# Reordering the edges of a matmul kernel: where x is loaded and turned at the start, the order of products in the first group and of the last quarters, and the slots for C

## The chip, the cores and the metric

The kernel runs on one core of a Trainium2 chip. The metric is device time in microseconds (us), smaller is better. A time here is the median of several executions, with the lowest and highest beside it. "Span" is the length of the one execution that was profiled; it comes out about 1.8 us below the time of the same execution.

In the profile lines, PE is TensorE's matmuls, PEld its loading of weights, DVE is VectorE, ACT ScalarE, POOL GpSimd, SP SyncE; a q after the name is that engine's queue, and xN a count. The "granted clock" is the share of TensorE's full clock that the profile shows as granted; "half clock" is a stretch where it is 0.50. A "chance wait" is one that some profiles of the same code show and others do not.

## The reference, cut to what matters

```python
def setup_inputs():
    B, S, D = 8, 2048, 2048
    return {"x": randn(B, S, D) as float32, "w": randn(D, D) as float32}

def reference(x, w):
    cs = np.cumsum(x, axis=1)
    diff = cs - (cs shifted by one row)      # which is x again
    return np.matmul(diff, w)
```

So the result is x (16384 rows of 2048) times w (2048 x 2048), in blocks of 128 rows.

## The kernel before

Three stages matter. **The first rows:** while w comes in, three row blocks of x are multiplied directly in bf16. Their x is loaded in four quarters, cast, turned by TensorE (transposes through two banks of PSUM) and copied out, by ScalarE and VectorE in turn.

```python
        load_x(0)
        ...
            for ko in range(KO - KQ):
                if h == 0 and ko % KQ == 2:
                    load_x(ko // KQ + 1)
                fetch(h, ko)                      # a block of w
                if h == 0 and ko % KQ == 0 and ko == 0:
                    turn_x(0)                     # 3 turns: cast, 4 transposes, copy
                taken(h, ko)                      # ScalarE casts it, VectorE takes its maximum
                for r in range(EARLY):
                    plain(h, r, ko)               # 2 matmuls for each of 3 row blocks
                if h == 0 and ko % KQ == 2:
                    turn_x(ko // KQ + 1)
```

**The groups:** all other rows go in groups of four blocks, with a fast two-by-two scheme in fp16: sums S1 to S4 of pieces of x, differences T1 to T4 of pieces of w, and seven products instead of eight. The first group (`group_plain`) makes whole products; in later ones three of the products are split once more (`inner_product`). Results gather in four float32 slots of C, `a` to `d`: `keep` copies a product from PSUM into a slot (ScalarE), `add` adds one to it (VectorE), `put` writes it out (a DMA from SyncE's queue). The rows of a later group are prepared on the side: `fetch_x` loads 1 MB, `weigh` measures the row's size on ScalarE *using a slot of C as a waste bin*, `scale_of` inverts the measure on VectorE, `ready` narrows to fp16 on ScalarE, `turn` transposes by DMA. The helper `after` fixes the order on each engine to the order of the calls.

```python
        C22 = new_c(d)                      # in group_plain
        keep(C22, Z, vg)
        ready(g + 4)
        turn(g + 4)
        fetch_x(g + 5)
        product(X, A21g, T3, False)
        add(C22, X, vg)
        put(C22, g + 1, 1)
        ...
        put(C12g, g, 1)
        weigh(h + 4, b)
        scale_of(h + 4)
        ...
        less_in(*in3)
        for t, X, slot, v in ((g, X, c, vg), (h, Y, b, vh)):
            product(X, parts(t + 1)[1], T4, False)
            ...
            put(C21, t + 1, 0)
        fetch_x(g + 8)
```

**The tail:** in the last group the final two quarters are made of seven small products sharing banks; the very last step is one addition over a full width of 1024 and one 512 KB write.

## Time and profile before

1523.6 us, median of 3 runs (1523.51 to 1524.18). By stage, in the profiled execution (span 1520.0):

| stage | from..to, us | length | what sets its end |
|---|---|---|---|
| first rows | 0..61.90 | 61.90 | TensorE, with pauses for turning x |
| fourth row block | 61.90..83.36 | 21.46 | ScalarE, busy 21.46 |
| first group to the first product S3 x T3 of the second | 83.36..153.51 | 70.15 | TensorE, with waits |
| rest of the passage, to inner product A3 | 153.51..169.91 | 16.40 | TensorE |
| steady groups, up to the end of the last full-width product | 169.91..1507.62 | 1337.71 | TensorE, without a pause |
| tail | 1507.62..1520.04 | 12.42 | last addition, write, end |

How to read it: two stages have TensorE continuous or nearly so, and there only fewer matmuls could help. The order of instructions shows 6904 matmuls before and after the change, so what can be won lies in the pauses. The lines that carry this are in the prediction below.

### The profile page before, as it was taken

What the parts mean: (1) busy time and instruction counts of PE and PEld (TensorE: products, weight loads), DVE (VectorE), ACT (ScalarE), POOL (GpSimd) and SP (SyncE); (2) the same over time, 40 slices, a digit from 0 to 9 for tenths busy, and PEclk for the clock granted to TensorE, in tenths of its full rate; (3) what the DMA queues carried; (4) which work ended last, traced back from release to release, by engine and by line L of the source; (5) the groups of instructions that cost most, each with busy time, mean ns of one, the idle gap of its engine ahead of it and who ended that gap; (6) DMA issues with size and microseconds to landing.
All of it is one profiled execution on the core that took longest, in us unless ns stands there. A gap on an engine that the chain in (4) does not pass through costs nothing.

```text
span 1520.0 us, 19095 instructions
## 1 busy us (share of the span) xinstructions
PE 1494.0 (98%) x6900; PEld 674.3 (44%) x6904; DVE 1104.8 (73%) x2066; ACT 861.2 (57%) x1102; POOL 10.0 (1%) x21
## 2 busy tenths in 40 slices
PE   6999999999999999999999999999999999999998
PEld 3443444444444444444444444444444444444443
DVE  7996776767776767776767776767776767777767
ACT  5865555655555565555565555565556565556551
POOL 0200000000000000000000000000000000000000
PEclk9999999999999999999999999999999999999999
DMA  9968789879788888888787787778887877887772
GB/s 365 362 189 225 208 243 222 228 229 245 214 247 207 238 231 241 219 240 223 223 241 233 224 235 216 226 228 241 234 237 206 232 230 232 238 236 222 220 206 111
DMA packets 321326, 351.49 MB, mean 231 GB/s; under 512 B 266832, under 2 KB 266832, under 8 KB 305232
## 3 DMA queue, kind: packets, MB, share of 16 engines
q1 hardware_dynamic: 319952, 346.08, 79.1%
q0 software_dynamic: 1280, 4.20, 0.8%
q8 instruction: 54, 0.88, 0.2%
q14 instruction: 40, 0.33, 0.1%
HBM read 150.99 MB, written 134.22 MB: 188 GB/s over the span
## 4 chain that ended last, share of the span: by engine, by line
PE 90%; DVE 0%; issue 0%; ACT 0%; ACTq 0%
PE b L366 54%; PE b L377 36%; DVE c L413 0%; ACT c L408 0%; DVE u L497 0%; DVE m L111 0%; DVE s L112 0%; ACTq L408 0%
## 5 line engine op out<-in xcount | busy, mean ns | idle before, releaser
L413 DVE SCALAR_TENSOR_TENSOR c<-b,u,c 128x512 f32<-128x512 f32 (+1 forms) x882 | 674.8, 800 | 237.8 <-ACT c L408 115.0
L408 ACT ACTIVATE c<-b,u 128x512 f32<-128x512 f32 x496 | 315.1, 680 | 278.9 <-PE b L366 183.7
L366 PE MATMUL b<-W,xT 128*128 128x512 f16 x2048 | 462.4, 379 | 0.6 <-ACT c L408 0.6
L366 PE MATMUL b<-W,W 128*128 128x512 f16 x1764 | 414.6, 381 | 0.9 <-ACT c L408 0.7
L105 ACT ACTIVATE c<-fin 128x2048 f16<-128x2048 f32 x92 | 175.7, 1910 | 246.9 <-DMA out_dram<-c 227.9
L366 PEld LDWEIGHTS <-xT 128*128 128x128 f16 x2048 | 200.3, 98 | 242.6 <-issue 1.0
L366 PEld LDWEIGHTS <-W 128*128 128x128 f16 x2016 | 197.7, 98 | 244.6 <-issue 4.9
L116 ACT ACTIVATE fin<-fin,s 128x2048 f16<-128x2048 f32 x123 | 246.3, 2002 | 90.0 <-issue 47.0
L377 PEld LDWEIGHTS <-W 128*128 128x128 f16 x1560 | 152.2, 98 | 186.8 <-issue 1.1
L377 PE MATMUL b<-W,W 128*128 128x512 f16 x810 | 219.8, 379 | 0.8 <-DVE c L413 0.8
L377 PE MATMUL b<-W,xT 128*128 128x512 f16 x720 | 179.9, 379 | 0.0
L377 PE MATMUL b<-inner,W 128*128 128x512 f16 x660 | 176.6, 379 | 0.0
L377 PEld LDWEIGHTS <-xT 128*128 128x128 f16 x960 | 93.9, 98 | 113.3
L472 DVE TENSOR_REDUCE m<-m 128x1 f32<-128x4 f32 x29 | 4.5, 157 | 104.0 <-ACT b L464 104.0
L366 PE MATMUL b<-W 128*128 128x512 f16 x252 | 76.0, 381 | 2.6 <-DVE W L422 2.5
L464 ACT ACTIVATE b<-fin 128x512 f32<-128x512 f32 x116 | 68.1, 587 | 12.6 <-DMA fin<-in_x_dram 11.9
L422 DVE TENSOR_TENSOR W<-W,xT 128x1024 f16<-128x1024 f16 x122 | 68.1, 559 | 3.2
L422 DVE TENSOR_TENSOR W<-xT,W 128x1024 f16<-128x1024 f16 x122 | 67.3, 552 | 0.0
L377 PE MATMUL b<-inner,xT 128*128 128x512 f16 x240 | 61.6, 379 | 0.0
L422 DVE TENSOR_TENSOR W<-xT,xT 128x1024 f16<-128x1024 f16 (+1 forms) x92 | 54.7, 595 | 0.0
L111 DVE TENSOR_SCALAR m<-m 128x1 f32<-128x1 f32 x124 | 18.5, 149 | 44.9 <-ACT c L105 43.8
L212 PE MATMUL b<-wb,xP 128*128 128x512 bf16 x188 | 44.3, 392 | 6.1 <-ACT wb L204 5.9
(56 smaller groups left out, 471.7 us busy)
## 6 DMA issues: line engine op xcount, KB each, us to landing
fin<-in_x_dram SPq DMA_DIRECT2D x124, 1024.0 KB, 5.4
out_dram<-c SPq DMA_DIRECT2D x248, 512.0 KB, 3.2
W<-in_w_dram SPq DMA_DIRECT2D x32, 512.0 KB, 9.3
W<-in_x_dram SPq DMA_DIRECT2D x12, 256.0 KB, 7.7
xT<-fin SPq DMA_TRANSPOSE x184, 5.0
out_dram<-o POOLq DMA_DIRECT2D x10, 256.0 KB, 5.4
out_dram<-wb POOLq DMA_DIRECT2D x6, 256.0 KB, 9.7
xP<-in_x_dram SPq DMA_DIRECT2D x1, 1024.0 KB, 7.4
```

Source lines behind the costliest of these rows:

```text
L105: return m, nc.scalar.activation(waste.bitcast(f16), xf, ABS, scale=1.0 / ROW, accum_out=m)
L111: nc.vector.tensor_scalar(m, m, TINY, None, MAX)
L116: return xh, nc.scalar.activation(xh, xf, COPY, scale=s)
L212: nc.tensor.matmul(ps[r][n], xP[:, r, ko, :], wb[h, ko][:, ds(n * NB, NB)], start=(ko == 0), stop=(ko == KO - 1),)
L366: nc.tensor.matmul(ps[n], a[k], b[k][:, n, :], start=(first and k == 0), stop=(k == KH - 1), skip_group_check=True,)
L377: nc.tensor.matmul(ps, a[k], b[k], start=(first and k == 0), stop=(k == 3), skip_group_check=True)
L408: after("act", lambda: nc.scalar.activation(c, p, COPY, scale=scale))
L413: "dve", lambda: nc.vector.scalar_tensor_tensor(c, p, scale, c, MUL, ADD)
L422: after("dve", lambda: nc.vector.tensor_tensor(dst.all, p.all, q.all, op))
L464: lambda: nc.scalar.activation(ps[i % 2], xf[:, at], ABS, scale=1.0 / ROW, accum_out=m4[:, i : i + 1],),
L472: after("dve", lambda: nc.vector.tensor_reduce(m, m4, AX.X, ADD))
```

## The change

Its intent: let the loads of w go ahead of three quarters of x so that products start on more of w; fill the passage between the first groups so that no engine stands behind a wait which its next piece of work does not need; keep products that share a bank apart in the tail and write the end in two halves. Cut to its core:

```diff
-                if h == 0 and ko % KQ == 2:
-                    load_x(ko // KQ + 1)
+                if h == 0 and ko == KQ:
+                    for q in range(1, 4):
+                        load_x(q)
...
+                if h == 0 and KQ <= ko < KQ + 3:
+                    turn_x(ko - KQ + 1)
...
@@ group_plain
         put(C12g, g, 1)
-        weigh(h + 4, b)
+        product(X, A22g, T4, False)
+        C21 = new_c(b)
+        keep(C21, X, vg)
+        put(C21, g + 1, 0)
+        weigh(h + 4, a)
...
-        C22 = new_c(b)
+        C22 = new_c(d)
         keep(C22, Z, vh)
-        weigh(g + 5, d)
+        weigh(g + 5, b)
...
@@ group, where it follows group_plain
-            weigh(h + 1, d)
-            ready(h + 1)
...
-            less_in3(*in3)
+            weigh(h + 1, c)
+            ready(h + 1)
             less_in(*in4)
-            less_in3(*in4)
...
         inner_product(A2, in2, banks, C11g, C11h, *u, between_2)
+        if second:
+            less_in3(*in3)
+            less_in3(*in4)
...
@@ the last group only (four_last): the small products in another order, and
-            add(halves(C21h), both(q), vh)
-            put(C21h, h + 1, 0)
+            for n in range(2):
+                at = ds(n * NB, NB)
+                add(C21h[:, at], q, vh)
+                nc.scalar.dma_start(out2[ds((h + 1) * P, P), at], C21h[:, at])
@@ the driver
-        slots = a, d, b, c
+        slots = (b, d, a, c) if g == PLAIN else (a, d, b, c)
```

More of the change, by code (lines that the diff above doesn't have):

```diff
@@ L240 @@
             for ko in range(KO - KQ):
-                if h == 0 and ko % KQ == 2:
-                    load_x(ko // KQ + 1)
+                if h == 0 and ko == KQ:
+                    for q in range(1, 4):
+                        load_x(q)
                 fetch(h, ko)
-                if h == 0 and ko % KQ == 0 and ko == 0:
+                if h == 0 and ko == 0:
                     turn_x(0)
+                if h == 0 and KQ <= ko < KQ + 3:
+                    turn_x(ko - KQ + 1)
                 taken(h, ko)
@@ L248 @@
                     plain(h, r, ko)
-                if h == 0 and ko % KQ == 2:
-                    turn_x(ko // KQ + 1)
             for ko in range(KO - KQ, KO):
@@ L605, in group_plain @@
         put(C22, g + 1, 1)
+        A22h = parts(h + 1)[1]
         S3h = sums(h, S4h)
@@ L629, in group_plain @@
         ready(g + 5)
+        turn(g + 5)
         product(Z, S4h, B22, False)
@@ L632, in group_plain @@
         put(C12h, h, 1)
+        fetch_x(g + 8)
         less_in(*in3)
-        for t, X, slot, v in ((g, X, c, vg), (h, Y, b, vh)):
-            product(X, parts(t + 1)[1], T4, False)
-            C21 = new_c(slot)
-            keep(C21, X, v)
-            if t == g:
-                turn(g + 5)
-            put(C21, t + 1, 0)
-        fetch_x(g + 8)
+        product(Y, A22h, T4, False)
+        C21 = new_c(c)
+        keep(C21, Y, vh)
+        put(C21, h + 1, 0)
     def group(g, X, Y, Z, V, a, b, c, d):
@@ L728, in between_3, with seven, four, four_last @@
                 ready(g + 5)
+        def seven():
+            product(Y, S3h, T3, False)
+            add(C22, Y, vh)
+            put(C22, h + 1, 1)
+        def four():
+            a11, a12, a22, s1, s2, s3, s4 = A4
+            Q1, Q2, Q4, t11, Q3, t21, t22 = in4
+            C21g, C21h = new_c(b), new_c(c)
+            product_in(X[0], a12, t21, False)
+            product_in(q, a11, t11, True)
+            product_in(X[1], s4, t22, False)
+            keep(C21g, X, vg)
+            turn(g + 5)
+            fetch_x(g + 8)
+            add(C21g[:, :NB], q, vg)
+            product_in(e, s1, Q1, True)
+            add(C21g[:, NB:], e, vg)
+            product_in(Y[0], a22, Q4, False)
+            keep(C21h, Y, vh)
+            product_in(q, s2, Q2, False)
+            add(C21g[:, NB:], q, vg)
+            put(C21g, g + 1, 0)
+            weigh(h + 5, d)
+            if g + 4 < END:
+                product(X, parts(g + 4)[0], B11, True)
+            add(C21h[:, NB:], e, vh)
+            product_in(q, s3, Q3, False)
+            scale_of(h + 5)
+            for t in (g + 4, h + 4) if g + 4 < END else ():
+                units[t] = unit(t)
+            add(halves(C21h), both(q), vh)
+            put(C21h, h + 1, 0)
+            ready(h + 5)
+        def four_last():
+            a11, a12, a22, s1, s2, s3, s4 = A4
+            Q1, Q2, Q4, t11, Q3, t21, t22 = in4
+            C21g, C21h = new_c(b), new_c(c)
+            product_in(q, a11, t11, True)
+            keep(C21g[:, :NB], q, vg)
+            product_in(X[0], a12, t21, False)
+            add(C21g[:, :NB], X[0], vg)
+            product_in(X[1], s4, t22, False)
+            keep(C21g[:, NB:], X[1], vg)
+            product_in(e, s1, Q1, True)
+            add(C21g[:, NB:], e, vg)
+            keep(C21h[:, NB:], Y[1], vh)
+            add(C21h[:, NB:], e, vh)
+            product_in(q, s2, Q2, False)
+            add(C21g[:, NB:], q, vg)
+            put(C21g, g + 1, 0)
+            product_in(Y[0], a22, Q4, False)
+            keep(C21h[:, :NB], Y[0], vh)
+            product_in(q, s3, Q3, False)
+            for n in range(2):
+                at = ds(n * NB, NB)
+                add(C21h[:, at], q, vh)
+                nc.scalar.dma_start(out2[ds((h + 1) * P, P), at], C21h[:, at])
         inner_product(A3, in3, banks, C12g, C12h, *u, between_3)
@@ L733, in group @@
         two()
-        product(Y, S3h, T3, False)
-        add(C22, Y, vh)
-        put(C22, h + 1, 1)
-        a11, a12, a22, s1, s2, s3, s4 = A4
-        Q1, Q2, Q4, t11, Q3, t21, t22 = in4
-        C21g, C21h = new_c(b), new_c(c)
-        product_in(X[0], a12, t21, False)
-        product_in(q, a11, t11, True)
-        product_in(X[1], s4, t22, False)
-        keep(C21g, X, vg)
-        turn(g + 5)
-        fetch_x(g + 8)
-        add(C21g[:, :NB], q, vg)
-        product_in(e, s1, Q1, True)
-        add(C21g[:, NB:], e, vg)
-        product_in(Y[0], a22, Q4, False)
-        keep(C21h, Y, vh)
-        product_in(q, s2, Q2, False)
-        add(C21g[:, NB:], q, vg)
-        put(C21g, g + 1, 0)
-        weigh(h + 5, d)
-        if g + 4 < END:
-            product(X, parts(g + 4)[0], B11, True)
-        add(C21h[:, NB:], e, vh)
-        product_in(q, s3, Q3, False)
-        scale_of(h + 5)
-        for t in (g + 4, h + 4) if g + 4 < END else ():
-            units[t] = unit(t)
-        add(halves(C21h), both(q), vh)
-        put(C21h, h + 1, 0)
-        ready(h + 5)
+        seven()
+        (four if g + 4 < END else four_last)()
     fetch_x(PLAIN + 3)
```

## The prediction

> **What bounds the kernel now.** I read the page first, then one table of busy time by stage, then the timeline wherever that table shows TensorE short of work.
>
> ```profile
> PE 1494.0 (98%) x6900; PEld 674.3 (44%) x6904; DVE 1104.8 (73%) x2066; ACT 861.2 (57%) x1102; POOL 10.0 (1%) x21
> ```
>
> The table's columns are the stretch, its length, busy time of each engine, granted clock, DMA share, GB/s.
>
> ```profile
> 0.00:61.90 61.90, 48.65 (x236) 22.54 (x240) 48.18 (x64) 38.12 (x46) 4.20 (x12) 1.00 0.96 372
> 61.90:83.36 21.46, 18.76 (x80) 7.82 (x81) 20.98 (x42) 21.46 (x23) 3.68 (x7) 0.92 0.97 292
> 83.36:140.25 56.89, 56.07 (x257) 24.75 (x255) 41.35 (x90) 27.87 (x32) 2.15 (x4) 1.00 0.78 216
> 140.25:153.51 13.26, 10.02 (x34) 3.80 (x34) 11.79 (x37) 9.27 (x18) 0.00 (x0) 0.74 0.76 180
> 153.51:1507.62 1354.11, 1354.11 (x6269) 612.77 (x6268) 976.16 (x1827) 761.86 (x984) 0.00 (x0) 1.00 0.80 226
> 1507.62:1520.00 12.38, 6.37 (x29) 2.64 (x27) 6.36 (x10) 2.64 (x4) 0.00 (x0) 0.95 0.41 169
> ```
>
> From 153.51 to 1507.62 us TensorE never pauses, at full clock: 1354 of 1520 us that no reordering shortens. A matmul costs 0.2157 us there (62 back to back took 13.54 us, the last one 0.38: (13.54 - 0.38) / 61). The order of instructions shows 6904 matmuls before and after. So the change can act only at the three edges: the load of w and x, the passage from the first group into the second, and the tail.
>
> The start, TensorE alone (start, length, what, count, and in brackets idle time with its releaser):
>
> ```profile
> 9.27 4.81 PE L212 MATMUL b<-wb,xP 128*128 128x512 bf16 x12 [1.34 <-ACT wb L204]
> 13.92 0.61 PE L183 MATMUL b<-eye,xb 128*128 128x128 bf16 x8
> 14.82 0.38 PE L183 MATMUL b<-eye,xb 128*128 128x128 bf16 x4 [0.29 <-DVE xP L188]
> 16.14 5.34 PE L212 MATMUL b<-wb,xP 128*128 128x512 bf16 x23 [0.94 <-ACT wb L204]
> 21.32 0.61 PE L183 MATMUL b<-eye,xb 128*128 128x128 bf16 x8
> 22.38 0.38 PE L183 MATMUL b<-eye,xb 128*128 128x128 bf16 x4 [0.45 <-ACT xP L186]
> 24.38 5.34 PE L212 MATMUL b<-wb,xP 128*128 128x512 bf16 x24 [1.62 <-ACT wb L204]
> ```
>
> Three times the products stop for a quarter of x to be turned: 13.92 to 16.14, 21.32 to 24.38, 29.56 to 31.79, together 7.5 us. From 40.74 to 61.90 TensorE is continuous, so it (not the DMA, although that is 96% busy) ends this stage.
>
> The passage, all engines:
>
> ```profile
> 139.49 1.91 ACT L105 ACTIVATE c<-fin 128x2048 f16<-128x2048 f32 x1 [3.20 <-DMA out_dram<-c]
> 141.52 0.15 DVE L111 TENSOR_SCALAR m<-m 128x1 f32<-128x1 f32 x1 [8.09 <-ACT c L105]
> 142.03 0.68 DVE L422 TENSOR_TENSOR W<-xT,xT 128x1024 f16<-128x1024 f16 x1
> 142.74 0.69 DVE L422 TENSOR_TENSOR W<-W,xT 128x1024 f16<-128x1024 f16 x1
> 142.76 0.66 PE L366 MATMUL b<-W 128*128 128x512 f16 x2 [2.51 <-DVE W L422]
> 143.87 2.40 ACT L408 ACTIVATE c<-b,u 128x512 f32<-128x512 f32 x4
> 144.59 0.59 PE L366 MATMUL b<-W,W 128*128 128x512 f16 x1 [0.73 <-ACT c L408]
> ```
>
> ScalarE waits until a slot of C has been written out, measures a row there, VectorE, idle for 8.09 us, scales that measure and only then forms S1 and S2, which TensorE needs. It idles 2.51 us, then runs at half clock from 143.18 to 150.01 (the table's 0.74). The 32 matmuls from there to 153.51 would have taken 6.9 us from 140.25; 6.4 us are lost.
>
> The tail:
>
> ```profile
> 1513.81 0.38 PE L377 MATMUL b<-W,W 128*128 128x512 f16 x1 [0.84 <-DVE c L413]
> 1514.87 1.28 DVE L413 SCALAR_TENSOR_TENSOR c<-b,u,c 128x1024 f32<-128x1024 f32 x1 [0.46 <-PE b L377]
> ```
>
> TensorE waits 0.84 us for a bank, then a double-width addition ends at 1516.15, and the write of 512 KB brings the end to 1520.0, 3.85 us later.
>
> **What the Trainium skill says.** "TensorE: Matmul & The Clock Gate", section "What's actually happening": the clock halves after an idle window of 3413 ns and returns after a busy one; windows run free of the kernel. The trace agrees: its changes at 13.48, 64.68, 68.09, 143.18 and 150.01 lie whole multiples of 3.413 apart. The same page, "Part 4: PE-mode transpose": transposes do not keep the clock up as products do. The trace agrees at 61.90, where 16 transposes fill 3.2 us between products and the clock halves at 64.68. "PSUM — Partial Sum Buffer", section "Engine vs sequencer instructions": the queues of ScalarE and VectorE are strict FIFO; here the 8.09 us show it, S1 standing behind a measure it does not use. "DMA: Bandwidth & Descriptors", section "Queues, rings and completion order": on each DMA engine descriptors are consumed in ring order. Here the transposes of x issued from 129.89 moved their 256-byte packets only at 135 to 137.5 us, behind a 1 MB load and two writes.
>
> **The change, part by part.** *Start.* w0 to w3 now precede the other three quarters of x. The first 12 products end at 13.92 as before; 12 more at 0.2157 end at 16.5. Then come all nine remaining turns in one block, on two banks used in turn. One turn by the trace: transposes at 21.32, copy 21.75 to 22.33, next transposes on that bank 22.38, so 1.06 us (ScalarE) or about 0.9 (VectorE), with VectorE also casting (0.36 each). Laid end to end by hand, the last ScalarE copy ends near 22.2. In ScalarE's new order the cast of w4 (1.04) stands behind it, so products resume near 23.3: one pause of 6.8 us for 7.5 in three, and product 61 begins at 23.3 + 36 x 0.2157 = 31.1 instead of 31.79: -0.7. But a pause of 6.8 us holds one whole window with transposes alone, which no pause before did. I expect half clock until 27.13 if the windows fall as now: 3.8 us at half speed, +1.9. Net +1.2, which I weigh at 0.85 against -0.7 without the drop: **+0.9**. TensorE stays the later one, so this passes on to the end.
>
> *Passage.* Taken away: the scale computed ahead of S1 and S2, and four-step subtractions of two sets (8 x 0.34 us of VectorE), which move behind the first inner product. X takes A22g with T4 directly after S4g, so the buffers of x free up at 115.5 rather than 129.75 us, and its C goes out earlier. VectorE should be done with the inner differences near 135.5 and then wait for the transposed x: the load ahead (to 133.5), one write (1.3) and the transpose (2.4) give 137.2, landed by 138; S1 and S2 end at 139.4, before TensorE asks at 140.25. The 2.51 us and the half clock go. ScalarE remains: its measure still waits for a write queued behind those transposes (about 139.2), then 2.0 + 0.5 + 2.0 for measure and narrowing, 1.26 for C11h, 2.6 for four measures, 0.65 for the first half of the C12g copy: 148.2. TensorE reaches the product that needs it at 140.25 + 6.9 = 147.15 and waits 1.1. Against 153.51 this gives 148.25: -5.3. VectorE is then about 1.2 us later, relative to TensorE, into the next inner product, where an addition must free a bank: +1.1. Net **-4.2**.
>
> *Tail.* Products sharing a bank stand further apart. I count a wait of 0.55 instead of 0.84, and the last addition in two halves of 0.69, the first written out at once; the half left moves 256 KB, 0.65 us less. Last matmul to end: -0.65; wait and order: -0.55. **-1.2**.
>
> Sum: 0.9 - 4.2 - 1.2 = -4.5; 1523.6 - 4.5 = **1519.1 us**.
>
> **Rivals.** (a) ScalarE as the new bound of the passage: if the slot's write lands 2 us later, TensorE waits 3 us and another half-clock window follows, which would leave 1522. For it: 4.05 and 3.20 us of ScalarE waits on writes of C in the profile; against: the write ahead of it is one fewer. (b) The start gains after all: the clock holds, or the early products fill the pauses better: 1517. For it: the short pauses kept full clock; against: 61.90. (c) The start's cold spell lasts two windows: 1520.5. (d) Everything at the start is hidden behind the DMA: against it stands the continuous TensorE from 40.74; it would give 1518.
>
> **Range and chances.** Start -1 to +2.7, passage -6.4 to -2, tail -1.5 to -0.6; not all extremes together: 1515.8 to 1522.3. Two per cent is 30 us, more than all idle time of TensorE at the edges that the change touches, so nearly all on "same".
>
> **What would show it.** Right: a clock drop near 20 us; products 61 on at about 33; no wait of TensorE for S1 and S2 near 140, no half clock at 143, but about 1 us for ScalarE near 147; from about 150 on the same continuous 1354 us; end 11.2 us after the last full-width product. Wrong: full clock through the start; a wait for transposed x near 140; a new gap after 153.

## The result, and the profile after

The changed kernel is correct. Its median is 1520.11 us (1519.01 to 1521.36, 4 runs) against 1523.89 us (1523.51 to 1525.45, 4 runs) of the kernel before in the same rounds. The ratio is 0.9974, 95% interval 0.9956 to 0.9991, which by the 2% rule counts as the same. Repeated on another chip, five runs gave 1519.90 us against 1522.79, ratio 0.9984 (0.9972 to 0.9997).

The page after, engine line:

```profile
PE 1493.7 (98%) x6904; PEld 674.1 (44%) x6904; DVE 1105.5 (73%) x2067; ACT 861.9 (57%) x1102; POOL 9.8 (1%) x21
```

TensorE's busy time fell by only 0.3 us (1494.0 before). What the span lost, it lost in pauses. Busy time is no measure of work here: half clock lengthens it, and that moved from the stretch with S1 and S2 (10.02 us busy before, 6.90 after) to the start (48.65 before, with four matmuls missing from the trace, 51.73 after).

Busy time by stage after; the columns are those of the table shown in the prediction (stretch, length, busy time of PE, PEld, DVE, ACT, POOL, granted clock, DMA share, GB/s):

```profile
0.00:62.94 62.94, 51.73 (x240) 23.36 (x240) 48.37 (x64) 38.92 (x46) 4.19 (x12) 0.95 0.94 365
...
84.41:143.80 59.39, 56.26 (x258) 25.00 (x257) 44.52 (x99) 30.27 (x35) 2.14 (x4) 1.00 0.75 206
143.80:150.70 6.90, 6.90 (x33) 3.11 (x32) 5.13 (x19) 6.74 (x14) 0.00 (x0) 1.00 1.00 235
150.70:1505.42 1354.72, 1354.45 (x6270) 612.82 (x6269) 980.07 (x1838) 761.84 (x985) 0.00 (x0) 1.00 0.80 226
1505.42:1517.60 12.18, 6.36 (x29) 2.64 (x27) 6.39 (x11) 2.64 (x4) 0.00 (x0) 0.91 0.43 172
```

Three things are to be seen. The first stage is longer by 1.04 us, and its granted clock has gone from 1.00 to 0.95. The stretch with S1 and S2 that took 13.26 us at clock 0.74 is now 6.90 us at 1.00, with TensorE busy all through. But the 59.39 us ahead of it hold 3.1 us without TensorE, where 56.89 us held 0.8 before: something was given back.

The start, TensorE alone (start, length, what, count, and in brackets the idle time before it with its releaser):

```profile
8.64 7.72 PE L212 MATMUL b<-wb,xP 128*128 128x512 bf16 x24 [0.45 <-ACT wb L204]
16.20 0.61 PE L183 MATMUL b<-eye,xb 128*128 128x128 bf16 x8
...
20.84 1.03 PE L183 MATMUL b<-eye,xb 128*128 128x128 bf16 x8 [0.85 <-DVE xb L180]
23.07 17.70 PE L212 MATMUL b<-wb,xP 128*128 128x512 bf16 x72 [1.19 <-ACT wb L204]
```

24 products run on end, then all 36 transposes in one block from 16.20 to 23.07 us, 6.87 us without a product. The 72 products that follow take 17.70 us; at 0.2157 us each they would take about 15.7. The clock column of the window below (0.50) says why:

```profile
20.32:27.15 6.83, 5.12 (x18) 2.31 (x19) 6.03 (x9) 5.66 (x7) 0.00 (x0) 0.50 1.03 410
```

The passage, lines of ScalarE, TensorE and VectorE:

```profile
127.42 1.26 ACT L409 ACTIVATE c<-b,u 128x512 f32<-128x512 f32 x2 [4.30 <-DMA out_dram<-c]
128.16 0.38 PE L367 MATMUL b<-W,W 128*128 128x512 f16 x1 [1.17 <-ACT c L409]
...
129.89 1.91 ACT L105 ACTIVATE c<-fin 128x2048 f16<-128x2048 f32 x1 [1.21 <-DMA out_dram<-c]
...
133.00 0.38 PE L367 MATMUL b<-W,xT 128*128 128x512 f16 x1 [0.87 <-DVE c L414]
133.66 10.30 PE L367 MATMUL b<-W,xT 128*128 128x512 f16 x47 [0.28 <-DVE c L414]
...
140.31 0.69 DVE L423 TENSOR_TENSOR W<-xT,xT 128x1024 f16<-128x1024 f16 x1 [1.13 <-DMA xT<-fin]
...
143.80 0.59 PE L367 MATMUL b<-W,W 128*128 128x512 f16 x2
```

The last two lines are the success: VectorE waits 1.13 us for the transposed x, forms S1 and S2 from 140.31 on, and TensorE takes them up at 143.80 without a wait. The first lines are the new loss. ScalarE's copy of C22 into slot d stands 4.30 us because the slot's earlier contents have not been written out; TensorE needs the bank that this copy frees and waits 1.17 us, and 0.20 more for the second bank of the pair. ScalarE's measure then waits 1.21 us for the write of slot b. VectorE stands behind that measure and frees its banks late: 0.87 and 0.28 us. Together 2.52 us.

Where that write stood can be read from SyncE's queue of the changed kernel (start, time taken to issue, what, count):

```profile
118.99 0.34 SPq L99 DMA_DIRECT2D fin<-in_x_dram  x1
119.37 1.86 SPq L419 DMA_DIRECT2D out_dram<-c  x3
```

Three writes of C follow immediately on a 1 MB load of x that stood ahead of them in the queue. SyncE stood 3.8 us before that load, for the transpose whose landing frees the load's buffer, while the addition that completes the first of the writes had ended at 116.28 us. The trace gives these writes a median of 8.7 us from issue to landing.

The tail:

```profile
1511.26 0.38 PE L378 MATMUL b<-W,W 128*128 128x512 f16 x1 [0.50 <-DVE c L414]
...
1512.39 1.41 DVE L414 SCALAR_TENSOR_TENSOR c<-b,u,c 128x512 f32<-128x512 f32 x2 [1.18 <-PE b L378]
1513.18 1.00 ACTq L796 DMA_DIRECT2D out_dram<-c  x2
```

TensorE's wait is 0.50 us instead of 0.84. The last addition, in two halves, takes 1.41 us against 1.28 in one piece.

Stage by stage, in the two profiles (lengths in us):

| stage | before | after | difference |
|---|---|---|---|
| first rows | 61.90 | 62.94 | +1.04 |
| fourth row block | 21.46 | 21.47 | +0.01 |
| first group, to S3 x T3 of the second | 70.15 | 66.29 | -3.86 |
| on to inner product A3 | 16.40 | 16.77 | +0.37 |
| steady groups | 1337.71 | 1337.95 | +0.24 |
| tail | 12.42 | 12.18 | -0.24 |
| span | 1520.04 | 1517.60 | -2.44 |

The second stage is a lesson of its own: its granted clock was 0.92 before and 1.00 after, and it took 21.46 and 21.47 us. ScalarE is busy for the whole of it, so a slow TensorE costs nothing there.

The medians of the same rounds differ by 3.78 us, and on the other chip by 2.89. One profile of each kernel cannot decide between such numbers, since executions of one kernel spread over several us. That is why the experiments below compare stages in many profiles rather than totals alone.

### The profile page after: what moved, and what is told of

Its sections match the earlier page's. It is cut to its first block, busy times and chain, and to the rows that moved or that the text cites. A ratio compares the mean times of both kernels' runs of the same rounds, so it can differ in the third digit from the quotient of the medians.

```text
span 1517.6 us, 19099 instructions
## 1 busy us (share of the span) xinstructions
PE 1493.7 (98%) x6904; PEld 674.1 (44%) x6904; DVE 1105.5 (73%) x2067; ACT 861.9 (57%) x1102; POOL 9.8 (1%) x21
```

## The experiments

Twelve runs were made (two of them repeat a kernel), each on one chip with the kernel before beside it. All gave correct results. "Passage" below is the time from the first product of the first group to the start of inner product A3 in the second: 86.55 us before, 83.06 after.

| run | median us (lowest to highest, runs) | kernel before | ratio (95%) | first rows end | passage | tail |
|---|---|---|---|---|---|---|
| start_alone | 1524.05 (1521.71 to 1525.18, 6) | 1522.84 | 1.0004 (0.9990 to 1.0018) | 63.65 | 86.53 | 12.40 |
| passage_alone | 1519.94 (1518.10 to 1522.33, 6) | 1522.84 | 0.9978 (0.9963 to 0.9992) | 61.77 | 82.94 | 12.41 |
| tail_alone | 1520.73 (1518.86 to 1526.15, 6) | 1522.84 | 0.9987 (0.9968 to 1.0005) | 61.76 | 90.12 | 12.05 |
| no_start | 1518.19 (1517.59 to 1519.48, 6) | 1522.84 | 0.9967 (0.9954 to 0.9980) | 61.75 | 82.88 | 12.17 |
| start_mixed | 1519.54 (1517.17 to 1523.12, 6) | 1524.38 | 0.9977 (0.9964 to 0.9990) | 61.29 | 82.74 | 12.17 |
| fetch_late | 1517.34 (1514.56 to 1518.45, 5) | 1524.38 | 0.9957 (0.9944 to 0.9970) | 64.75 | 80.08 | 12.18 |
| mixed_fetch | 1519.37 (1516.18 to 1522.32, 6) | 1524.38 | 0.9971 (0.9956 to 0.9985) | 61.10 | 86.96 | 12.18 |
| tail_sp | 1518.0 (1 run, state unknown) | 1524.38 | none | 62.27 | 82.75 | 12.01 |
| after_again | 1519.90 (1518.52 to 1521.38, 5) | 1522.79 | 0.9984 (0.9972 to 0.9997) | 63.48 | 84.34 | 12.17 |
| after_fetch | 1516.68 (1514.99 to 1518.28, 5) | 1522.79 | 0.9960 (0.9948 to 0.9973) | 63.89 | 80.03 | 12.18 |
| fetch_late_again | 1517.22 (1514.81 to 1518.30, 5) | 1522.79 | 0.9963 (0.9950 to 0.9975) | 61.48 | 79.92 | 12.16 |
| tail_whole | 1519.75 (1518.32 to 1520.73, 5) | 1522.79 | 0.9980 (0.9967 to 0.9994) | 64.55 | 82.91 | 12.09 |

The three right-hand columns are each from one profile. Theory: the passage gains, because S1 and S2 no longer stand behind the measure; the start costs about 1 us, by a cold spell; the tail gains little. Rivals: the start hides behind the DMA; the passage only moves its wait; the tail's gain is eaten by ScalarE's queue.

### Each part alone, and the whole without the start

`start_alone`: the kernel before with only the first hunk, the three `load_x` at `ko == KQ` and `turn_x(ko - KQ + 1)` after them.

> The kernel before with the new order of loads of x and w alone. My theory: the long pause for nine turns halves TensorE's clock once, and as TensorE ends this stage, the loss is passed on: 1 us slower than before (0.5 to 2), one half-clock stretch of about 6.8 us near 20 us, the products of the first rows ending near 62.9 us instead of 61.9. Rival: the load is paced by the DMA, so the clock does not matter here: 0.0, or faster by the 0.7 us by which the pauses got shorter.

In time it is not to be told from the kernel before. In its profile the first rows end at 63.65 us, 1.75 later than in the profile of before, with half clock from 20.93 for 6.83 us. The old wait for S1 and S2 is there again (2.63 us, up to 145.59). That the passage takes 86.53 us, as before, is a coincidence: it holds a chance wait of 0.89 us near 92 us, and its half clock lasts 3.41 us instead of 6.83.

`passage_alone`: the kernel before with only the edits in `group_plain`, `group` and the slots.

> The kernel before with the new order and slots of the first group alone. My theory: all of the change's gain is here: 3.5 us faster than before (2.5 to 4.5), no half clock near 143 us, but 2.5 us of new waits of TensorE around 127 to 133 us for a slot of C. Rival: the gain comes from elsewhere, this part gives under 1.5 us.

The ratio's interval lies wholly below 1. The passage shrinks to 82.94 us, with no half clock in it, and the new waits are the same as in the whole change: 0.86 and 0.20 us behind ScalarE at 126 us, 0.86 and 0.28 behind VectorE at 131. So both gain and loss belong to this part.

`tail_alone`: the kernel before with only `four_last`.

> The kernel before with the new last quarters alone. By my prediction 1.2 us faster; by the one profile of the changed kernel only 0.2 us faster, because the end follows the last packet by 2.0 us instead of 1.5. A mean difference over 0.8 us would say that the one profile misled.

In time this one is inconclusive, its own runs lie 7 us apart. The ratio means about 2.0 us less, over the 0.8 that the expectation had set as a sign that the one profile misled, but its interval reaches from -4.9 to +0.8 us and so holds the 0.2 of the profile as well. Its profile shows a chance wait of 2.50 us for transposed x near 90 us, so its passage of 90.12 us says nothing of the tail. The tail itself took 12.05 us for 12.42.

`no_start`: the changed kernel with the old order of loads.

```diff
-                if h == 0 and ko == KQ:
-                    for q in range(1, 4):
-                        load_x(q)
+                if h == 0 and ko % KQ == 2:
+                    load_x(ko // KQ + 1)
```

> The changed kernel with its order of loads taken back. If the parts add up: the change without its loss at the start, 4.5 to 5 us faster than before, that is 0.5 to 1.5 us faster than the changed kernel. Rival (the start is worth nothing or gains): equal to or slower than the changed kernel's 3.8 us.

1518.19 us, and first rows at 61.75 again. Its ratio 0.9967 is below the changed kernel's 0.9974 and 0.9984, but the intervals overlap; the times alone do not show that the new start costs anything.

### The cold spell at the start

`start_mixed`: the changed kernel, but the nine turns are threaded one by one between the products of w2, w3 and w4, in an order fixed on TensorE, so that the block of transposes never forms.

```diff
+                for ko in range(2, 4):
+                    taken(0, ko)
+                    for r in range(EARLY):
+                        turn_one(ko - 1, r)      # one turn,
+                        plain(0, r, ko)          # two products, chained in this order
```

> The changed kernel, loads in its new order, but the nine turns no longer in one block: two products of w2, w3 or w4 stand between each turn and the next, in forced order. If the halved clock is what the new start costs: full clock through 16 to 28 us, products of the first rows ending at 60.5 to 61.9 us (62.9 in the changed kernel), total 1 to 2 us below the changed kernel. Rival: the loss is the pause itself, or casts that come late: the clock stays up and the products still end near 63.

First rows end at 61.29 us, so the block of transposes did cost. The other two expectations failed: the total is not 1 to 2 us below the changed kernel's (ratios 0.9977, and 0.9974 and 0.9984), and the clock still halves for one window, from 22.05 us, and the reason stands in TensorE's timeline of this run:

```profile
21.29 0.59 PE L230 MATMUL b<-wb,xP 128*128 128x512 bf16 x2 [2.75 <-ACT wb L222]
```

TensorE waits 2.75 us for the cast of w4, which now stands behind ScalarE's copies. So the mixing was not worth its code.

The old order was not free of this either. In one profile with the old start (the run `tail_whole`, told below), the second of its three pauses for turning x fell so that the clock halved too. TensorE's timeline there, and then the two windows around the drop:

```profile
25.48 6.90 PE L212 MATMUL b<-wb,xP 128*128 128x512 bf16 x24 [1.62 <-ACT wb L204]
```

```profile
21.84:25.25 3.41, 1.57 (x16) 0.98 (x15) 2.61 (x5) 1.94 (x3) 0.00 (x0) 1.00 1.04 395
25.25:28.66 3.41, 3.18 (x8) 1.17 (x8) 3.41 (x6) 3.02 (x4) 0.00 (x0) 0.50 1.04 412
```

These 24 products took 5.34 us in the kernel before and 6.90 here, behind the same pause. Eight profiles have the old order of loads: their first rows end at 61.48, 61.75, 61.76, 61.77, 61.90, 62.27, and, with such a drop, 64.55 and 64.75 us, mean 62.53. Four have the new order: 62.94, 63.48, 63.65 and 63.89 us, all with half clock for 6.83 us from 20.3 to 21.3 on, mean 63.49. The new order makes certain what the old one met in two of eight, and costs an estimated 1.0 us (the difference of the two means), too little for these timings to show.

What the two have in common can be read from the traces. In all 14 profiles the clock changes only at whole multiples of 3.413 us from its first change. When the profiles are cut into such windows, the time of products in a window tells what follows, and TensorE's busy time as a whole does not: the four blocks fill a window with 1.89 to 1.98 us of transposes and no product, and the clock halves, while in `tail_sp` the window 20.85 to 24.26, with 1.84 us of both but 1.01 of products alone, keeps it. In `tail_whole` 0.74 us of products fell into the window, in `fetch_late` 0.51. Over all 14 profiles, every window at full clock with at most 0.96 us of products was followed by half clock, and every one with 1.24 us or more by full clock; of five between, the one with 1.19 us in `tail_alone` was followed by half clock and the others were not. This second pause is 3.1 us long in all eight profiles of the old order; luck is where the windows' limits fall in it.

### The new waits in the passage

`fetch_late`: the changed kernel with the old order of loads and one line moved in `group_plain`: the 1 MB load of row g + 5 is issued after the writes of C22 and C12g, no longer ahead of them.

```diff
         turn(g + 4)
-        fetch_x(g + 5)
         product(X, A21g, T3, False)
         add(C22, X, vg)
         put(C22, g + 1, 1)
...
         put(C12g, g, 1)
+        fetch_x(g + 5)
```

> The changed kernel with the old order of loads at the start, and in the first group one load of x issued after two writes of C instead of before them. If TensorE's new waits of 2.2 us (near 125 to 132 us) come from a slot of C whose write stands behind that load: they go, ScalarE waits for no write there, and it is 1.5 to 2.5 us faster than the same without this edit (1518.2), near 1516. Rival: the slot is only what ended the wait last and another wait (the transposed x, VectorE) takes over: under 0.7 us.

The passage takes 80.08 us instead of `no_start`'s 82.88, and TensorE's four waits are gone. Only its start had bad luck, as told above. In all it took 0.85 us less than `no_start`, where 1.5 to 2.5 was expected, but the two ran on different chips; the next run compares on one.

`after_fetch`: the changed kernel with this one move and nothing else, on one chip with the changed kernel (`after_again`) and with `fetch_late` again.

> The changed kernel with one edit: the 1 MB load of the next but one rows is issued after the write of C12g, not before the writes of the passage. If the queued write of C costs the 2.5 us of TensorE's waits between 126 and 134 us: from the first group's product to the inner product A3 of the next group 80.1 to 80.5 us instead of 83.1, and about 2.5 us less in all than the changed kernel, 1517.6; half clock at the start stays. Rival, the load is then later and a wait for transposed x near 140 us takes its place: 83 us, no gain.

> The changed kernel itself, again, beside the candidates on the same chip. Expected as before: ratio to the kernel before 0.9974 (0.9956 to 0.9991), about 1520 us. The profile: half clock near 20.3 to 27.1, and two new waits of TensorE between 126 and 134 us.

> Old order of loads with the new passage, the new tail and the later load, again, to hold its 1517.3 us against the changed kernel on one chip. If the start's half clock costs about 1 us and the queued write 2.5: ratio 0.9955 or below, 3 us faster than the changed kernel. Rival, its first result was luck of the random waits near 90 us: 1518.5 to 1520.

The passage takes 80.03 and 79.92 us. (The 84.34 of `after_again` holds a chance wait of 1.55 us, told below, besides the new waits.) SyncE's queue in `after_fetch`, to set beside the one shown of the changed kernel:

```profile
116.14 1.44 SPq L419 DMA_DIRECT2D out_dram<-c  x2
120.01 0.34 SPq L99 DMA_DIRECT2D fin<-in_x_dram  x1
```

Two writes leave at 116.14, 3.2 us earlier, and the writes of C in this window, three again, land with a median of 5.0 us instead of 8.7. How much of the gain is the earlier issue and how much the shorter landing is not separated. Then ScalarE and TensorE at the place where the waits were:

```profile
124.30 1.26 ACT L409 ACTIVATE c<-b,u 128x512 f32<-128x512 f32 x2 [0.24 <-PE b L367]
...
127.77 1.46 PE L367 MATMUL b<-W,W 128*128 128x512 f16 x6
...
131.22 10.67 PE L367 MATMUL b<-W,xT 128*128 128x512 f16 x48
```

ScalarE's copy into slot d waits 0.24 us, for the product itself, and TensorE not at all. In time `after_fetch` takes 1516.68 us against the changed kernel's 1519.90 on the same chip, 3.2 us less; its highest run, 1518.28, is below the changed kernel's lowest, 1518.52. The rival, a later load that brings a wait for transposed x near 140 us, did not occur: VectorE waited 0.94 us there, and TensorE not. `fetch_late_again` held its first result, but at ratio 0.9963, a little above the 0.9955 expected, and its advantage of 1 us over `after_fetch` by the better start did not show in the times (1517.22 against 1516.68). Its profile, on the other hand, was the shortest of all (span 1513.0), as one with neither cold start nor chance wait should be. Both versions beat the kernel before and the changed one.

`mixed_fetch`: `start_mixed` and the moved load together.

> Both edits on the changed kernel. If they are independent: the sum, near 1515 to 1516.5. If the start is only as good as the old one, equal to fetch_late. Rival: slower than fetch_late by over 1 us, which would say that loading x early costs something besides the clock.

A miss as a combination: 1519.37 us. Its profile had the largest of the chance waits, 4.04 us for transposed x at 89 us, with 6.83 us of half clock after it, which is why its passage reads 86.96. This wait showed in 4 of 14 profiles, with the old start and the new (0.89, 1.55, 2.50 and 4.04 us). In the last three, SyncE took 2.8 to 4.4 us to issue that transpose (the one near 83 us), in the others 1.8 to 2.3. What delays it is not settled. It is one reason why executions of one kernel differ by several us.

### The tail

`tail_sp`: `no_start` with the two final writes issued from SyncE instead of ScalarE.

```diff
-                nc.scalar.dma_start(out2[ds((h + 1) * P, P), at], C21h[:, at])
+                nc.sync.dma_start(out2[ds((h + 1) * P, P), at], C21h[:, at])
```

> The changed kernel with the old order of loads, the last two half writes issued by SyncE instead of ScalarE. Read from the profile, last full-width product to end of the span: 12.17 us with ScalarE. If ScalarE's queue is what ate the gain: 11.6 us or less. Rival: a write of 256 KB ends no sooner after its last packet on either queue, 12.0 to 12.3.

12.01 us of tail instead of 12.17: ScalarE's queue accounts for 0.16 us at most, not for the missing gain.

`tail_whole`: `no_start` with the new order of products, but the last addition and its write in one piece.

```diff
-            for n in range(2):
-                at = ds(n * NB, NB)
-                add(C21h[:, at], q, vh)
-                nc.scalar.dma_start(out2[ds((h + 1) * P, P), at], C21h[:, at])
+            add(halves(C21h), both(q), vh)
+            put(C21h, h + 1, 0)
```

> Old order of loads, new passage, new order of products in the tail, but the last addition and its write in one piece, as in the kernel before. From the end of the last full-width product to the end of the run the kernel before takes 12.4 us, the halves 12.17. If the halves gain nothing and the new order gains 0.3 us by its shorter bank wait (0.50 for 0.84): 12.05 to 12.1 here, the same as with halves. Rival, that the halves do gain 0.65 us and the new order loses some elsewhere: 12.7 to 12.8 here.

12.09 us, as the reading that the halves gain nothing had it. TensorE's wait is 0.50 us here too, and VectorE is back to one addition:

```profile
1513.80 1.28 DVE L413 SCALAR_TENSOR_TENSOR c<-b,u,c 128x1024 f32<-128x1024 f32 x1 [1.17 <-PE b L377]
```

So the small gain of the tail comes from the order of products alone. From the last full-width product to the last matmul's end it is 7.21 us before, 6.86 in the changed kernel and 6.87 here; from there to the end of the run 5.21, 5.32 and 5.22. Splitting cost 0.1 us in eight of the nine profiles that have halves on ScalarE's queue (5.30 to 5.32), and nothing in `tail_alone` (5.19).

## Why the prediction was right or wrong

The class and the range held, the class almost by necessity, as the prediction says itself: 1519.1 us was predicted, 1520.11 measured, within 1515.8 to 1522.3. By its own steps:

| step | predicted | in the two profiles |
|---|---|---|
| start | +0.9 | +1.04 |
| passage | -4.2 | -3.49 (-3.86 and +0.37) |
| tail | -1.2 | -0.24 |
| the rest | 0 | +0.25 |
| sum | -4.5 | -2.44 |

**What bounds it: right.** The steady groups took 1337.7 to 1338.0 us in every profile, whatever was changed around them, and every gain or loss of the start and the passage passed on to the end.

**The start: right, in size and mechanism.** The pause is 6.87 us, worked out as 6.8; half clock came at 20.32 and ended at 27.15, foreseen for "near 20" and 27.13; its reading at 61.90, that transposes do not hold the clock up, could not tell them from idle time there, but the block shows it; product 61 began at 32.83, foreseen near 33. One clause was too strong: that no pause of the old order held a cold window. In two of eight profiles one did. This does not overturn the sum, because the mean of all profiles gives +1.0.

**The passage: mechanism right, one term misplaced and mis-sized.** "The 2.51 us and the half clock go": they did. S1 and S2 ended at 141.7 us (139.4 were worked out, 140.4 with the later start), and TensorE asked for them at 143.80. The -5.3 was 6.4 us of losses less 1.1 of new waiting. The new waiting was 2.52 us, so -6.4 + 2.5 = -3.9, and -3.86 was measured. The wait foreseen near 147, ScalarE behind its measure, never came. In its place stood waits near 127 and 132 us, for a write of C. The step that failed is the one that followed C only through the writes near 139 us; it did not ask which slot the moved C22 now used, nor that its old contents were queued behind a load. The moved load shows the size: 83.06 to 80.03 us, 3.0 us. The load's place is thus tested; that the slot matters is read from the wait alone, since no run gave C22 its old slot back. The 1.1 us given back in the next inner product was 0.37.

**The tail: the direction held, the size was wrong.** The term "wait and order: -0.55" measured -0.35, with a bank wait of 0.50 where 0.55 was said. The term "last matmul to end: -0.65" measured +0.11. Half the data did leave sooner: from issue to last packet 1.77 us (1513.83 to 1515.60) against 2.27 for the whole (1516.22 to 1518.49), -0.50. But the last addition ended 0.19 us later after the last matmul, 1.52 against 1.33. And the end of the run came 2.00 us after the last packet instead of 1.55, +0.45. The whole write of `tail_whole` has 1.55 again. Of the 0.45, 0.39 lies between the last packet and the signal that the write has landed (0.74 us for the halves, 0.35 for the whole), and 0.06 in the closing instructions after it (1.26 against 1.20). So the second half took 2.51 us from issue to landing where the whole took 2.62. With the issue 0.03 us closer to the addition, -0.50 + 0.19 + 0.45 - 0.03 = +0.11. Why the halves' signal comes later after the last packet is not settled; it is no property of ScalarE's queue alone, since SyncE's halves took 1.9 to the end, 0.78 of it to the signal.

**The rivals.** Of (a), ScalarE as a new bound, the idea was right and the place wrong: the waits behind writes were 2.5 us and brought no cold window. (b) fell on the cold spell, (d) on the start's end in every profile. Of (c), the cold spell lasted two windows, which is what the +1.2 had counted.

## What to carry to other kernels

When work is moved so that it uses another buffer, ask for that buffer's last reader, and where *its* transfer stands in the queue: here one load ahead of finished writes cost 3 us, about as much as the change had won. A block of transposes as long as two clock windows halved TensorE's clock in all four profiles that had it, while shorter pauses only risk it. Splitting a last write pays only if its fixed end does not grow; measure the end, not the bytes.

## What the Trainium skill lacked or had wrong

- "TensorE: Matmul & The Clock Gate", section "Why this matters for your kernels", advises against idle gaps of TensorE of more than about 3 us between bursts of matmuls. In the old order the gap between products is 3.1 us (21.32 to 24.38 before, 22.42 to 25.48 in `tail_whole`), with transposes in part of it, and it halved the clock in two of eight profiles. So a gap of about the page's figure can go either way. The page does not say how much work in a window counts as enough: here windows of 3.41 us with up to 0.96 us of products lost the clock, and those with 1.24 or more kept it.
- "DMA: Bandwidth & Descriptors", section "Anatomy of one DMA — SWDGE (gpsimd) path", gives a fixed cost of about 2.0 us, mostly the receipt of the last byte, as roughly constant. The last writes here go through other queues, so they do not contradict it. For them the time from the last packet to the landing signal was 0.35 us after one write of 512 KB (packets of 4096 bytes, 159 ns each), and 0.74 (ScalarE) or 0.78 (SyncE) after two of 256 KB (2048 bytes, 86 ns each).
- None of the pages read says that the time SyncE spends on issuing a DMA transpose varies from run to run: the same one took 1.8 to 4.4 us in 14 profiles.
